# Swapping the halves of rotated heads: four copies on ACT or four transfers

## The chip, the cores and the metric

The kernel runs on one core of a Trainium2 chip, as one launch. The time is that of the device for one execution, in microseconds (us), lower is better. The profiled executions are separate runs, each with its own time. TensorE is called PE in the profile (PEld its weight loads), VectorE DVE, ScalarE ACT, GpSimd POOL; SP is the engine that issues most transfers. Each engine works through its own queue in order and waits for the others at semaphores.

## The reference, cut to what matters

A two-layer model on 256 tokens of width 1024: layer one is a gated recurrence, layer two an attention, each followed by a feed-forward block. The change lies in the attention, where keys and queries are normalised per head (64 channels) and rotated:

```python
def apply_rope(x, cos, sin):
    x1, x2 = jnp.split(x, 2, axis=-1)
    ...
    return jnp.concatenate([x1 * cs - x2 * sn, x2 * cs + x1 * sn], axis=-1)
...
ks = apply_rope(rms_norm(k_sel, k_norm[1]), cos, sin)
kw = apply_rope(rms_norm(k_win, k_norm[2]), cos, sin)
...
q = rms_norm(proj[..., :NSA_Q_WIDTH].reshape(B, S, NSA_HEADS, NSA_HEAD_DIM), q_norm)
q_rope = apply_rope(q, cos, sin)
```

The first half of a head's channels needs the second half at the same token, and the other way round.

## The kernel before, in words

Activations lie with channels on the 128 partitions and the 256 tokens along the free dimension, so a tile of two heads has four blocks of 32 partitions: half, half, half, half. All weights stream from HBM in tiles of 1 MB (`raw`, four buffers, issued on SP's queue in a fixed order, `SCHED`); each is split by ACT into a rounded part (`wh`, L319) and by DVE into the rest (`wl`, L320), and each product is three matmuls (L507 to L509). A raw buffer is loaded anew when whatever read it is done.

The order of the attention's work is written out in the list `ORDER["nsa"]` (L68), but a scheduler sets the final place of each instruction on each engine, by its own costs; the decorator `first` (L187) lends some steps a priority, the rotation a lower one (-15).

The steps that matter here, in the order of the text:

- Keys: two products give `k` for the branches sel and win. ACT writes `hsqk` (squares, L1075) and `huk` (the raw heads, L1076), 128x512 for each branch.
- `rotate` (L1004): `us` gets the heads with the halves swapped (L1010); DVE multiplies the heads by gain and cosine into `KR` or `QR` (L1013), `us` by the swapped gain and the signed sine (L1014), and adds both (L1015). It is called twice for keys (`usk`, `huk`) and four times for queries (`usq`, `huq`), each time for two tiles of two heads.
- `head_norm` (L1017): PE sums the squares (`hs`, L1025); ACT and DVE take the reciprocal root (`hry`, `hrt`, `hrr`, L479 to L486: logarithm, exponent, square, a Newton step), which is split in two (L502, L503); PE spreads it over the channels (`hb`, L1034 and L1035); DVE multiplies (`KR` or `QR`, L1036, and `QN`, L1038). Once for the keys, once for each two query tiles.
- Compression: blocks `Z` (ACT and DVE, L1163 and L1165) and `D` (DVE, L1168) are the stationary side of `cmp` (PE, L1186, 32 matmul records against the two `w1` tiles in `raw`, 32 against `w1late`), whose result runs through a sigmoid (`sg`, `hid`), a transpose (`hidt`), `kc`, `kcsq` (ACT, L1216), `kcms` and `vc`.
- Query tiles: `nq` products; ACT copies them to `huq` (L998) and squares them to `hsqq` (L1000); then rotation and norm. `gates` is a further product, copied to `gu` (L1242) and transposed (`gt`, L1245).
- `v` products (L802 to L804) take `h`, which ACT and DVE compute meanwhile; `css` is the softmax over compressed blocks (L1261 to L1271), its transpose `pct` (PE, L1274); then come the scores `s` (L1291), their maxima and exponents `Pt` (DVE L1296, ACT L452), transposes `ptt` and products `po`. PE fills gaps with `adapsg` and `adapsss` (L408), products for later modulation, fed from `raw` tiles.

Of the kernel before, what the change touches and what calls it, by code (L numbers as in the profile page):

```python
# [186 lines left out]
def first(name):  # L187

    def wrap(f):
        def g(self, *a, **k):  # L190
            n = PRI.get(name, 0)
            if not n:
                return f(self, *a, **k)
            with self.tc.high_priority(offset=n):
                return f(self, *a, **k)
        return g
    return wrap


class K:  # L200
# [802 lines left out]
    @first("rot")  # L1003
    def rotate(self, u, gain, swap, kr, name):  # L1004

        nc = self.nc
        us = self.s2.tile([P, 2, S], F32, tag="us", bufs=2, name=f"us{name}")
        for b in range(4):
            d, e = 32 * b, 32 * (b ^ 1)
            nc.scalar.dma_start(us[d:d + 32], u[e:e + 32])  # L1010
        cs = self.c("cos")[:, None, :].to_broadcast([P, 2, S])
        sn = self.c("sin")[:, None, :].to_broadcast([P, 2, S])
        nc.vector.scalar_tensor_tensor(kr, u, gain, cs, op0=ALU.mult, op1=ALU.mult)  # L1013
        nc.vector.scalar_tensor_tensor(us, us, swap, sn, op0=ALU.mult, op1=ALU.mult)  # L1014
        nc.vector.tensor_tensor(kr, kr, us, op=ALU.add)  # L1015
# [454 lines left out]
```

## Time and profile before

| | |
|---|---|
| median of 3 runs | 744.41 us (742.66 to 746.78) |
| the profiled execution's own time | 748.7 us |
| its span, first to last instruction | 746.9 us |
| mean granted clock of TensorE | 0.986 |
| PE busy | 718.2 us, 96% |
| DVE busy | 587.3 us, 79% |
| ACT busy | 409.7 us, 55% |
| transfers of L1010 | 24 of 64 KB each, issued from 396.68 to 457.28 us |

The profile is of one execution. A timeline row gives start, duration, engine, line and operation, output from input, how many were merged, and in brackets the time that the engine had been idle and what ended it. A waits row gives the waiter, whom it waited for, the sum, how often and the longest. A windows row gives for each stretch its length, the busy time of PE, PEld, DVE, ACT and POOL with the number of instructions, the granted TensorE clock, the share of the transfer engines and GB/s. A group row gives the busy time, the mean duration in ns and the idle time ahead with its releasers. ACTq and SPq are the sequencers of ACT and SP, which issue transfers.

### The profile page before, as it was taken

What the parts mean: (1) busy time and instruction counts of PE and PEld (TensorE: products, weight loads), DVE (VectorE), ACT (ScalarE), POOL (GpSimd) and SP (SyncE); (2) the same over time, 40 slices, a digit from 0 to 9 for tenths busy, and PEclk for the clock granted to TensorE, in tenths of its full rate; (3) what the DMA queues carried; (4) which work ended last, traced back from release to release, by engine and by line L of the source; (5) the groups of instructions that cost most, each with busy time, mean ns of one, the idle gap of its engine ahead of it and who ended that gap; (6) DMA issues with size and microseconds to landing.
All of it is one profiled execution on the core that took longest, in us unless ns stands there. A gap on an engine that the chain in (4) does not pass through costs nothing.

```text
span 746.9 us, 14669 instructions
## 1 busy us (share of the span) xinstructions
PE 718.2 (96%) x5892; PEld 632.0 (85%) x5892; DVE 587.3 (79%) x1221; ACT 409.7 (55%) x796; POOL 0.4 (0%) x5
## 2 busy tenths in 40 slices
PE   3999998999999999999998999999999999999997
PEld 2999986789999999988897797555799888888886
DVE  5996989369899788889677897688689868776642
ACT  4348968267645454544464563757666555565330
POOL 0000000000000000000000000000000000000000
PEclk9999999799999999999999899999999999999999
DMA  8898736555479797889636544455665556756710
GB/s 343 329 351 344 270 109 274 224 226 175 164 283 393 267 362 267 345 307 355 256 131 214 208 160 142 169 195 202 226 221 174 208 188 229 264 183 233 268 43 22
DMA packets 26566, 174.05 MB, mean 233 GB/s; under 512 B 3201, under 2 KB 4609, under 8 KB 6018
## 3 DMA queue, kind: packets, MB, share of 16 engines
q1 hardware_dynamic: 24912, 170.80, 61.8%
q10 hardware_dynamic: 1586, 2.32, 1.0%
q8 instruction: 46, 0.75, 0.4%
q14 instruction: 22, 0.18, 0.1%
HBM read 170.48 MB, written 1.05 MB: 230 GB/s over the span
## 4 chain that ended last, share of the span: by engine, by line
PE 87%; DVE 5%; ACT 3%; DMA 2%; issue 1%; ACTq 0%; DVEq 0%
PE ffo L519 11%; PE ff L507 6%; PE ff L509 6%; PE ff L508 6%; PE ffo L520 6%; PE ff L519 5%; PE po L1348 3%; PE ff L520 2%; PE adapsss L408 2%; PE ptt L1331 2%; PE s L1291 2%; DVE wl L320 1%; PE cmp L1186 1%; PE hg_g L507 1%; PE hg_i L802 1%; PE q L508 1%
## 5 line engine op out<-in xcount | busy, mean ns | idle before, releaser
L319 ACT CAST wh<-raw 128x1024 fp32r<-128x1024 f32 x201 | 208.8, 1049 | 156.1 <-PE ffo L519 47.9
L320 DVE TENSOR_TENSOR wl<-raw,wh 128x1024 fp32r<-128x1024 f32 x201 | 244.4, 1222 | 56.3 <-ACT wh L319 55.4
L519 PE MATMUL ffo<-g,wh 128*128 128x512 f32 x352 | 123.5, 394 | 0.0
L520 PE MATMUL ffo<-g,wl 128*128 128x256 f32 x352 | 99.1, 282 | 0.0
L507 PE MATMUL ff<-hh,wh 128*128 128x256 f32 (+1 forms) x352 | 99.0, 282 | 0.0
L508 PE MATMUL ff<-hl,wh 128*128 128x256 f32 (+1 forms) x352 | 98.8, 281 | 0.0
L509 PE MATMUL ff<-hh,wl 128*128 128x256 f32 (+1 forms) x352 | 98.8, 281 | 0.0
L519 PEld LDWEIGHTS ffo<-g,wh 128*128 128x128 f32 x352 | 66.2, 188 | 15.3
L382 DVE CUSTOM_DVE_ANT_0 junk<-raw,crep 128x1024 f32<-128x1024 f32 x64 | 78.0, 1219 | 0.4
L508 PEld LDWEIGHTS ff<-hl,wh 128*128 128x128 f32 x352 | 66.4, 189 | 0.1
L509 PEld LDWEIGHTS ff<-hh,wl 128*128 128x128 f32 x352 | 66.4, 189 | 0.0
L507 PEld LDWEIGHTS ff<-hh,wh 128*128 128x128 f32 x352 | 66.2, 188 | 0.0
L520 PEld LDWEIGHTS ffo<-g,wl 128*128 128x128 f32 x352 | 66.1, 188 | 0.0
L519 PE MATMUL ff<-h,wh 128*128 128x512 f32 x152 | 54.2, 395 | 0.0
L520 PE MATMUL ff<-h,wl 128*128 128x256 f32 x152 | 42.6, 280 | 0.0
L452 ACT ACTIVATE Pt<-Pt,nm 128x128 f32<-128x128 f32 x64 | 28.2, 443 | 13.7 <-DVE nm L1300 13.6
L519 PEld LDWEIGHTS ff<-h,wh 128*128 128x128 f32 x152 | 28.7, 189 | 6.8 <-DVE h L626 0.2
L677 DVE SCALAR_TENSOR_TENSOR x<-ffo,mod,x 128x256 f32<-128x256 f32 x32 | 15.4, 482 | 18.4 <-PE ffo L520 18.1
L520 PEld LDWEIGHTS ff<-h,wl 128*128 128x128 f32 x152 | 28.6, 188 | 0.0
L502 ACT CAST g<-fg 128x256 fp32r<-128x256 f32 x44 | 17.8, 404 | 17.4 <-DVE fg L971 16.6
L1296 DVE CUSTOM_DVE_ANT_0 Pt<-s,cst 128x128 f32<-128x128 f32 (+1 forms) x64 | 19.0, 351 | 4.1 <-PE s L1291 4.0
L625 ACT ACTIVATE h<-t,mod 128x256 fp32r<-128x256 f32 x16 | 7.7, 506 | 24.1 <-DVE t L624 24.1
(455 smaller groups left out, 1747.0 us busy)
## 6 DMA issues: line engine op xcount, KB each, us to landing
raw<-in_w SPq DMA_DIRECT2D x158, 1024.0 KB, 5.2
w1late<-in_w SPq DMA_DIRECT2D x2, 1024.0 KB, 9.3
x<-in_x SPq DMA_DIRECT2D x2, 512.0 KB, 4.9
usq<-huq ACTq DMA_DIRECT2D x16, 64.0 KB, 4.2
out<-x SPq DMA_DIRECT2D x8, 128.0 KB, 1.9
cst<-in_cst ACTq DMA_DIRECT2D x1, 558.0 KB, 6.9
raw<-in_w SPq DMA_DIRECT2D x1, 512.0 KB, 3.2
usk<-huk ACTq DMA_DIRECT2D x8, 64.0 KB, 6.6
```

What stands on the lines that cost most here:

```text
L319: nc.scalar.copy(wh, u)
L320: nc.vector.tensor_tensor(wl, u, wh.bitcast(F32), op=ALU.subtract)
L382: nc.vector.tensor_tensor_reduce(out=junk, in0=t[:, h * D:(h + 1) * D], in1=self.crep, scale=1.0, scalar=0.0, op0=ALU.mult, op1=ALU.add, a ...
L452: r = nc.scalar.activation(out, in_, func, **kw)
L502: self.nc.scalar.copy(hi, v)
L507: mm(ps, lhsT=wh, rhs=hh, start=first, stop=False)
L508: mm(ps, lhsT=wh, rhs=hl, start=False, stop=False)
L509: return mm(ps, lhsT=wl, rhs=hh, start=False, stop=last)
L519: mm(ps, lhsT=w[k][0], rhs=b, start=k == 0, stop=False)
L520: mm(ps[:, 0], lhsT=w[k][1], rhs=b[:, 0], start=False, stop=k == n - 1)
L1296: nc.vector.tensor_tensor_reduce(out=Pt[half][:, br, o:o + n], in0=ps[half][:, br], in1=cs[:, S - n:], scale=1.0, scalar=-3e38, op0=ALU.ad ...
L1348: nc.tensor.matmul(po[64 * half:64 * half + 64, t], lhsT=w[:, half], rhs=rhs, start=n == 0, stop=n == len(steps) - 1, tile_position=(0, 64 ...
```

## The change

One line of `rotate`. Each of the four blocks of 32 partitions by 512 elements went from `u` to its swapped place in `us` as a transfer issued on ACT's queue; now ACT copies it itself.

```diff
         us = self.s2.tile([P, 2, S], F32, tag="us", bufs=2, name=f"us{name}")
         for b in range(4):
             d, e = 32 * b, 32 * (b ^ 1)
-            nc.scalar.dma_start(us[d:d + 32], u[e:e + 32])
+            nc.scalar.copy(us[d:d + 32], u[e:e + 32])
```

The scheduler then places other instructions differently too; SP's order stays as it was. Four shifts matter to the text. Three are shown, as the rows of the built program give them (line, operation, output from input, size).

ACT, ahead of the key norm's last step on ACT (`hry` from `hrr`), before; `usk_5025` is the second key branch:

```order
L1075 ACTIVATE hsqk_4957<-u,sw 128x256
L1076 ACTIVATE huk_4958<-u,sw 128x256
L452 ACTIVATE hry<-hs,eps 128x256
L1010 DMA usk_5025<-huk_4958 32x512
L452 ACTIVATE hry<-hry 128x256
L1010 DMA usk_5025<-huk_4958 32x512
L482 ACTIVATE hrt<-hry 128x256
L1010 DMA usk_5025<-huk_4958 32x512 x2
L502 CAST hry<-hrr 128x256
L1163 ACTIVATE Z_5075<-u,sw 64x128 x4
```

And now, at the same place:

```order
L319 CAST wh_0_5272<-raw_4966 128x1024
L1075 ACTIVATE hsqk_4957<-u,sw 128x256
L1076 ACTIVATE huk_4958<-u,sw 128x256
L452 ACTIVATE hry<-hs,eps 128x256
L1010 COPY usk_5025<-huk_4958 32x512
L452 ACTIVATE hry<-hry 128x256
L1010 COPY usk_5025<-huk_4958 32x512
L482 ACTIVATE hrt<-hry 128x256
L1010 COPY usk_5025<-huk_4958 32x512 x2
L1163 ACTIVATE Z_5075<-u,sw 64x128 x4
L319 CAST wh_0_5320<-raw_4976 128x1024
L502 CAST hry<-hrr 128x256
```

The four Z operations and two weight casts (5272 is that of `gates`, 5320 the first of the second query tile) stood behind `hry<-hrr` and stand ahead of it now. On PE, nine matmuls of `gates` and two of the second query tile have moved ahead of `hb` along with them, and on DVE both operations that write the second `D` (L1168) stand behind the split of the norm (`hrt`, L503) and ahead of both `hb` multiplies (L1036); before, the first of these and the second key's L1014 stood ahead of them, and that key's L1015 between them. The second key's L1014 and L1015 stand ahead of that split now.

DVE, in the softmax over compressed blocks, before; `usq_5608` is the third query tile's:

```order
L1264 TENSOR_TENSOR css<-css,cmx 128x256
L320 TENSOR_TENSOR wl_1_5729<-raw_5328,wh_1_5728 128x1024
L1266 TENSOR_REDUCE cmx<-css 128x16
L553 CAST hh_6461<-zero 128x8
L554 CAST hl_6462<-zero 128x8
L1267 RECIPROCAL cmx<-cmx 128x16
L1270 TENSOR_TENSOR css<-css,cst 128x256
L1269 TENSOR_TENSOR cmx<-cmx,G 128x16
L1014 SCALAR_TENSOR_TENSOR usq_5608<-usq_5608,cols,cst 128x512
L1271 TENSOR_TENSOR css<-css,cmx 128x256
L1015 TENSOR_TENSOR QR<-QR,usq_5608 128x512
```

And now:

```order
L1264 TENSOR_TENSOR css<-css,cmx 128x256
L1014 SCALAR_TENSOR_TENSOR usq_5608<-usq_5608,cols,cst 128x512
L1266 TENSOR_REDUCE cmx<-css 128x16
L1015 TENSOR_TENSOR QR<-QR,usq_5608 128x512
L1267 RECIPROCAL cmx<-cmx 128x16
L1270 TENSOR_TENSOR css<-css,cst 128x256
L1269 TENSOR_TENSOR cmx<-cmx,G 128x16
L553 CAST hh_6461<-zero 128x8
L554 CAST hl_6462<-zero 128x8
L1271 TENSOR_TENSOR css<-css,cmx 128x256
```

The multiply of `usq` (L1014) stood right ahead of the last `css` step (L1271) and now stands ahead of the sum (L1266).

PE, inside the first `v` product, as the difference (+ is now, - was); `adapsg_5999` is a product whose other 31 matmuls stand far behind, `raw_5494` its weights:

```order
-L804 MATMUL v_5485<-wh_1_5490,h_5234 128x256
+L408 MATMUL adapsg_5999<-raw_5494,c_110 32x256
 L1245 MATMUL gt<-cst,gu 128x128
 L1025 MATMUL hs<-hsqq_5155,cst 32x256 x2
 L1025 MATMUL hs<-hsqq_5381,cst 32x256 x2
 L1245 MATMUL gt<-cst,gu 128x128
+L804 MATMUL v_5485<-wh_1_5490,h_5234 128x256
```

One `adapsg` matmul stands ahead of `gt` and the query norm's `hs` now. Fifteen matmuls of the third query tile that stood ahead of this place are done behind the `v` product instead.

Last, on ACT, three of the second query tile's four copies stand ahead of `kcsq` and the fourth ahead of `gu`; of its transfers two were issued ahead of `kcsq`.

## The prediction

> **What bounds the kernel now.** The page comes first: it says which engine the span is made of.
>
> ```profile
> span 746.9 us, 14669 instructions
> ...
> PE 718.2 (96%) x5892; PEld 632.0 (85%) x5892; DVE 587.3 (79%) x1221; ACT 409.7 (55%) x796; POOL 0.4 (0%) x5
> ...
> usq<-huq ACTq DMA_DIRECT2D x16, 64.0 KB, 4.2
> ...
> usk<-huk ACTq DMA_DIRECT2D x8, 64.0 KB, 6.6
> ```
>
> PE is busy nearly everywhere, so this edit, which takes no matmul away, can only win where PE waits or runs slowly. The 24 transfers take 4.2 and 6.6 us from issue to landing (medians). Next, the longest waits of PE in the stretch 395 to 480 us, where all 24 lie (in total, times, longest):
>
> ```profile
> PE hb L1034 <- ACT hry L502: 3.1, 1, 3.1
> PE pct L1274 <- DVE css L1271: 1.7, 1, 1.7
> PE cmp L1186 <- DVE D L1168: 1.4, 1, 1.4
> ...
> ```
>
> None names a transfer. The timelines of DVE, ACT and PE show what stands behind three of them (start, duration, in brackets the idle time ahead and its releaser):
>
> ```profile
> 406.85 0.75 DVE L1014 SCALAR_TENSOR_TENSOR usk<-usk,cols,cst 128x512 f32<-128x512 f32 x1 [3.39 <-DMA usk<-huk]
> ...
> 412.42 0.75 DVE L1014 SCALAR_TENSOR_TENSOR usk<-usk,cols,cst 128x512 f32<-128x512 f32 x1
> 413.08 0.69 DVE L1168 TENSOR_TENSOR D<-Z,cols 128x512 f32<-128x512 f32 x1
> ...
> 457.39 0.75 DVE L1014 SCALAR_TENSOR_TENSOR usq<-usq,cols,cst 128x512 f32<-128x512 f32 x1 [1.81 <-DMA usq<-huq]
> 458.06 0.42 DVE L1271 TENSOR_TENSOR css<-css,cmx 128x256 f32<-128x256 f32 x1
> ```
>
> ```profile
> 409.54 0.40 ACT L502 CAST hry<-hrr 128x256 fp32r<-128x256 f32 x1 [5.53 <-DMA usk<-huk]
> 409.86 1.66 ACT L1163 ACTIVATE Z<-u,sw 64x128 f32<-64x128 f32 x4
> ...
> 412.01 2.44 ACTq L1010 DMA_DIRECT2D usq<-huq  x4
> ```
>
> ```profile
> 401.73 0.62 PE L1025 MATMUL hs<-hsqk,cst 128*32 128x256 f32 x2 [0.58 <-ACT hsqk L1075]
> ...
> 406.66 0.28 PE L509 MATMUL nq<-hh,wl 128*128 128x256 f32 x1
> 410.00 0.50 PE L1034 MATMUL hb<-hry,rsel 128*128 128x256 f32 x2 [3.06 <-ACT hry L502]
> ...
> 413.82 5.64 PE L1186 MATMUL cmp<-raw,D 128*64 128x256 f32 x29 [1.40 <-DVE D L1168]
> ...
> 419.31 3.83 PE L1186 MATMUL cmp<-w1late,D 128*64 128x256 f32 x31
> ```
>
> ACT and DVE stand in order behind transfers that have not landed: the key norm waits behind them, so hb does; D and css stand behind a usk or usq multiply in DVE's queue. Last, the windows view, in steps of 3.41 us laid on the two dips of the granted clock (PEclk is the number ahead of the DMA share):
>
> ```profile
> 404.63:408.05 3.42, 2.31 (x20) 2.10 (x18) 1.16 (x2) 0.00 (x0) 0.00 (x0) 1.00 1.00 349
> 408.05:411.46 3.41, 1.46 (x7) 1.00 (x8) 1.76 (x5) 1.88 (x6) 0.00 (x0) 1.00 0.27 82
> 411.46:414.87 3.41, 2.01 (x11) 1.35 (x12) 3.05 (x5) 1.39 (x4) 0.00 (x0) 0.50 0.24 58
> 414.87:418.29 3.42, 3.42 (x20) 1.90 (x18) 3.42 (x6) 2.56 (x3) 0.00 (x0) 0.50 0.08 19
> 455.83:459.24 3.41, 1.68 (x15) 1.28 (x14) 1.84 (x4) 0.08 (x1) 0.00 (x0) 1.00 0.93 335
> 459.24:462.65 3.41, 3.34 (x13) 1.91 (x10) 2.88 (x17) 0.00 (x0) 0.00 (x0) 0.50 0.05 13
> ```
>
> A window with 1.40 us of idle PE or more (3.41 less 2.01, 1.46 or 1.68) is followed by one at half clock; one with 1.11 us (3.42 less 2.31) is not. So the waits are paid twice.
>
> **The change part by part.** *Price of a copy.* No row shows 32 partitions by 512 from SBUF. The ACT groups of the stretch, by form:
>
> ```profile
> L319 ACT CAST wh<-raw 128x1024 fp32r<-128x1024 f32 x16 | 16.6, 1050 | 7.7 <-PE nq L508 3.2 <-DMA usq<-huq 2.0 <-PE kv L508 1.7
> ...
> L1163 ACT ACTIVATE Z<-u,sw 64x128 f32<-64x128 f32 x8 | 3.3, 407 | 1.0 <-DVE u L668 0.9
> ...
> L502 ACT CAST hh<-t 128x256 fp32r<-128x256 f32 x8 | 2.9, 403 | 0.7 <-DVE t L639 0.6
> ...
> L998 ACT COPY huq<-nq 128x512 f32<-128x512 f32 x4 | 2.3, 575 | 1.6 <-PE nq L509 1.6
> ```
>
> Between 256 columns (403 ns) and 1024 (1050 ns) the straight line gives 0.62 us at 512. Four Z copies, which change partitions, take 1.66 us (4 x 0.407 is 1.63), so I let nothing overlap and take 0.62. The low end is 0.48 (the 575 ns copy with the roughly 0.1 us by which neighbours on ACT overlap); the high end 1.05, the cast of double length, should moving across partitions halve the rate. All 24: 14.9 us of ACT. Four are 2.5 us where ACT's queue took 2.44 us to issue four transfers, so ACT is held no longer than before; what goes is the landing.
>
> *hs and hb.* ACT's rows ahead of the key norm:
>
> ```profile
> 397.32 0.16 ACT L667 COPY sw<-k 128x1 f32<-128x1 f32 x1 [0.68 <-ACT huk L1076]
> ...
> 398.19 0.52 ACT L1075 ACTIVATE hsqk<-u,sw 128x256 f32<-128x256 f32 x1 [0.71 <-DVE u L668]
> ...
> 399.64 0.16 ACT L667 COPY sw<-k 128x1 f32<-128x1 f32 x1 [0.23 <-issue]
> ...
> 401.17 0.51 ACT L1075 ACTIVATE hsqk<-u,sw 128x256 f32<-128x256 f32 x1 [1.37 <-DVE u L668]
> ```
>
> Four copies and the moved gates cast (2.48 + 1.05 = 3.53) fill 2.99 us of idle here (0.68 + 0.71 + 0.23 + 1.37): hsqk, and hs with it, come 0.54 later, and PE's wait of 0.58 becomes 1.12. hs ended at 402.35 (401.73 + 0.62) and now ends at 402.89. From there ACT does three functions of hry (0.42 each), four copies (2.48), Z (1.66) and the nq cast (1.05) before the hry cast: 6.45 us, so that starts at 409.34 instead of 409.54, and hb, 0.46 behind it, at 409.80. PE, 0.54 later with its nq row (free at 407.32), now has nine gates matmuls first (9 x 0.12 = 1.07, to 408.39), waits for the nq cast (to 409.34), does two matmuls (0.24) and waits for hb: 1.17 us idle instead of 3.06. Both waits together: 3.64 to 2.29, a gain of **1.35**. It is ACT, no longer a transfer, that is late next.
>
> *cmp.* In DVE's queue the first hb multiply and the second key's L1014 stood ahead of D. Now that key's work is done while ACT works towards hry, and D stands right behind hrt's split (L503), which starts with hry's cast done, at 409.74: half a microsecond of L503 and one D operation of 0.69 end near 410.8, while PE does hb until about 411. Gain **1.40**, with little cover: 0.2 us.
>
> *First dip.* 29 records at 5.64/29 = 0.194 us against 3.83/31 = 0.124 at full clock: 29 x 0.071 = **2.05**, if no window idles 1.40 us any more.
>
> *pct.* The usq multiply moves ahead of the exponent's sum in DVE's queue, and its data comes 2.5 us of copies behind huq instead of a landing; ACT, which does css's exponent too, idles there and has room for both. The wait of 1.74 us goes: **1.74**. Late next are the nq matmuls, after which the v matmuls fill PE until css is done.
>
> *Second dip.* Eight s records in the dip and eight at full clock:
>
> ```profile
> 458.90:461.32 2.42, 2.42 (x8) 1.67 (x10) 0.57 0.18 44
> 468.06:469.45 1.39, 1.39 (x8) 0.68 (x8) 1.00 0.00 0
> ```
>
> 2.42 - 1.39 = **1.03**; these feed DVE's maxima and the exponents that PE waits for later, and the next eight overlap with DVE, so I count one set. The Trainium skill, "TensorE: Matmul & The Clock Gate", section "Part 1: The HAM clock gate", lets the clock fall to half after an idle window of about 3.4 us. By that rule a window half busy, like 455.83 to 459.24, should not count and the sum would be 1.03 smaller; the row shows half clock behind it, and the row decides.
>
> *What the copies cost.* Three of them now stand ahead of kcsq, which had only 1.02 us of idle before it (ACT's, PE's and SP's timelines, and the landings of weight loads between 415 and 440 us):
>
> ```profile
> 433.70 0.23 ACT L1216 ACTIVATE kcsq<-kc 128x64 f32<-128x64 f32 x1 [1.02 <-PE kc L1213]
> ...
> 438.11 0.27 PE L1245 MATMUL gt<-cst,gu 128*128 128x128 f32 x1
> ...
> 431.24 0.33 SPq L296 DMA_DIRECT2D raw<-in_w  x1
> ...
> DMA to landing us min/median/max: 4.9/9.2/12.0
> ```
>
> 3 x 0.62 - 1.02 = 0.84 later, and one more copy (0.62) ahead of gu; PE's v matmuls, which covered both, need h casts from the same queue. Bounds 0 and 1.46; I take **1.2** lost, near the upper, as 15 nq matmuls that filled PE here move behind.
>
> *At nothing:* SP's order is unchanged; raw buffers come free earlier because the gates cast does (cover: the transfers landed in time before). Without the cover, a wait for weights, see below.
>
> Sum: 1.35 + 1.40 + 2.05 + 1.74 + 1.03 - 1.2 = **6.4 us**. The profiled execution took 748.7 us (span 746.9) and would take 742.3; it was 4.3 us above the median of the three runs (742.66 to 746.78), so I take the difference off the median: 744.4 - 6.4 = **738.0 us**.
>
> **The rivals.**
>
> *Copies at the upper bound.* At 1.05 us, eight of them ahead of hb add 8 x 0.43 = 3.4 us to that wait, the first dip stays (2.05), and kcsq and gu lose another 1.7: 6.4 - 7.2 = -0.8, **745.2 us**, no change. For it: the rows at hand have other shapes. Against: the Z copies change partitions at no visible price.
>
> *The clock stays low.* The new wait at hs (1.12) and that at hb (1.17) lie between the 1.11 that did no harm and the 1.40 that did. Then 2.05 stays lost: **740.1 us**, still faster.
>
> *The second dip has another cause.* Should the half clock at 459.24 come of something else than the half-idle window ahead of it, it stays: **739.0 us**. That is how the Trainium skill's clock-gate section would have it; four windows of this trace speak against it, three idle ones and one that was not idle enough.
>
> *Slower: a matmul ahead of its weights.* One adapsg matmul (L408) moves from far behind into the middle of the v product, just ahead of gt and hs. PE serves in order. Its raw tile was issued only at 431.24, and loads of that stretch took 4.9 to 12.0 us to land. By then the kernel has gained 3.6 us (1.35 + 1.40 + 2.05 - 1.2), and the 15 nq matmuls that move behind are another 1.8, so gt's place comes near 432.7 (438.11 - 5.4). The load's buffer comes free with the last v weights, which gain the 3.6 and some 1.5 more, as their own raw tile is loaded earlier: issue near 426. At 4.9 us it lands at 431, in time. At 12.0 it lands at 438, PE idles 5.3 us, and two windows at half clock lose up to 3.4: 6.4 - 8.7 = -2.3, **746.7 us**; it decides once the landing takes over 9.7 us (3.0 us idle and the 3.4 are the whole gain), and with copies at their upper bound too it makes 754. Against it: three loads, not four, queue together then.
>
> **How the numbers follow.** Forecast 0.58; copies at the upper bound, or another loss that ACT's load gives back, 0.17; clock stays low 0.13; the second dip's other cause 0.05; weights late 0.07. About 0.5% (3.7 us) is what a measurement of this kernel can tell from no change, so faster means under 740.7 us, slower over 748.1. The clock's rival lies 0.6 us inside that bound, so two thirds of it count as faster (0.09), with the forecast and the second dip's other cause: 0.72. Of late weights most counts as slower, since its price has no firm upper end, 0.05; the rest, 0.23, is no change. Range: downward, copies at 0.48 save 8 x 0.14 = 1.1 at hb and a cover without loss 1.2, which gives 735.7, and about 1 us more if the last wait of the list, 0.58 at hs, also goes with a ready hsqk: 734.5. Upward it takes in the clock's rival and most of the way to the first: 743.5.
>
> **What would show it.** Right: no wait of ACT or DVE for usk or usq; PE's wait at hb about 1.2 us and at cmp none; PEclk 1.00 from 405 to 425 and near 455; ACT's busy time up by 15 us; L1010 at 0.62 us. Wrong: L1010 near 1 us, PEclk still 0.50 behind hb, a wait of PE at adapsg or kcms of several us, or gt at an unchanged 438.1 us (about 432.7 expected).

## The result, and the profile after

The changed kernel takes 741.16 us (median of eight runs, 738.19 to 742.57), the kernel before, in the runs beside it, 747.00 (eight runs, 742.66 to 749.11): a ratio of 0.9923, 95% interval 0.9894 to 0.9951, or 5.8 us. In a second measurement (the last run below), with other runs of the kernel before, it was 0.9889 (0.9854 to 0.9923). The forecast was 6.4 us less, 738.0 us, with a range of 734.5 to 743.5. The measured time lies in it, 3.2 us above the forecast; 2.6 of these come from the kernel before, which takes 747.00 us here and took 744.41 in the three runs that the forecast started from. The profiled execution took 741.87 us. Its page begins:

```profile
span 740.1 us, 14648 instructions
...
PE 716.4 (97%) x5892; PEld 631.1 (85%) x5892; DVE 586.5 (79%) x1221; ACT 424.6 (57%) x820; POOL 0.4 (0%) x5
```

ACT is busy 14.9 us longer (409.7 before), what 24 copies of 0.62 us make. PE's waits in the same stretch, 395 to 480 us:

```profile
PE nq L507 <- ACT wh L319: 1.0, 1, 1.0
PE hs L1025 <- ACT hsqk L1075: 1.0, 1, 1.0
PE s L1291 <- DVE mx L1296: 0.4, 1, 0.4
```

hb, pct and cmp are gone from the list, and so is a wait of 0.6 at ptt. ACT, DVE and PE around the key norm, one timeline each:

```profile
404.88 1.24 ACT L1010 COPY usk<-huk 32x512 f32<-32x512 f32 x2
406.15 1.68 ACT L1163 ACTIVATE Z<-u,sw 64x128 f32<-64x128 f32 x4
407.85 1.04 ACT L319 CAST wh<-raw 128x1024 fp32r<-128x1024 f32 x1
408.80 0.40 ACT L502 CAST hry<-hrr 128x256 fp32r<-128x256 f32 x1
```

```profile
406.56 0.74 DVE L1014 SCALAR_TENSOR_TENSOR usk<-usk,cols,cst 128x512 f32<-128x512 f32 x1
...
409.24 0.43 DVE L503 TENSOR_TENSOR hrt<-hrr,hry 128x256 fp32r<-128x256 f32 x1 [0.99 <-ACT hry L502]
409.58 1.29 DVE L1168 TENSOR_TENSOR D<-Z,cols 128x512 f32<-128x512 f32 x2
```

```profile
408.95 0.39 PE L507 MATMUL nq<-hh,wh 128*128 128x256 f32 x1 [1.03 <-ACT wh L319]
...
411.23 3.52 PE L1186 MATMUL cmp<-raw,D 128*64 128x256 f32 x29
...
431.62 0.33 PE L1245 MATMUL gt<-cst,gu 128*128 128x128 f32 x1
```

ACT does the hry cast without idle time ahead of it (5.53 us before); the second key's L1014 waits for nothing; the 29 cmp records take 3.52 us instead of 5.64; gt comes 6.49 us earlier. The windows view shows the clock:

```profile
408.16:411.57 3.41, 2.62 (x16) 2.00 (x18) 2.29 (x5) 3.38 (x7) 0.00 (x0) 1.00 0.64 267
411.57:414.98 3.41, 3.41 (x34) 3.18 (x32) 3.41 (x6) 3.12 (x4) 0.00 (x0) 1.00 0.00 0
452.54:455.95 3.41, 2.95 (x10) 1.07 (x8) 3.33 (x21) 1.60 (x5) 0.00 (x0) 1.00 0.00 0
455.95:459.36 3.41, 3.41 (x15) 3.12 (x15) 2.46 (x13) 3.41 (x17) 0.00 (x0) 0.50 0.00 0
```

The dip behind hb is gone. The one near 456 us is still there in this profile, now behind a window with only 0.46 us idle.

### The profile page after: what moved, and what is told of

Its sections match the earlier page's. It is cut to its first block, busy times and chain, and to the rows that moved or that the text cites. A ratio compares the mean times of both kernels' runs of the same rounds, so it can differ in the third digit from the quotient of the medians.

```text
span 740.1 us, 14648 instructions
## 1 busy us (share of the span) xinstructions
PE 716.4 (97%) x5892; PEld 631.1 (85%) x5892; DVE 586.5 (79%) x1221; ACT 424.6 (57%) x820; POOL 0.4 (0%) x5
## 3 DMA queue, kind: packets, MB, share of 16 engines
HBM read 170.48 MB, written 1.05 MB: 232 GB/s over the span
## 4 chain that ended last, share of the span: by engine, by line
PE 88%; ACT 5%; DVE 4%; issue 1%; DMA 1%; ACTq 0%
PE ffo L519 11%; PE ff L507 6%; PE ff L509 6%; PE ff L508 6%; PE ffo L520 6%; PE ff L519 5%; PE po L1348 3%; PE adapsss L408 2%; PE ff L520 2%; PE ptt L1331 2%; PE s L1291 2%; PE q L508 1%; PE hg_i L802 1%; PE hg_g L507 1%; DVE wl L320 1%; PE nso L507 1%
```

## The experiments

Times are medians; each ratio is to the runs of the kernel before made beside it (747.1 to 747.8 us). Where an edit adds lines, later lines are numbered one or two higher in its rows.

**Keys alone.**

```diff
-            nc.scalar.dma_start(us[d:d + 32], u[e:e + 32])
+            (nc.scalar.copy if name[0] == "k" else nc.scalar.dma_start)(us[d:d + 32], u[e:e + 32])
```

> The keys' eight blocks are copied by ACT, the queries' sixteen stay transfers. Theory (a landing that stands in the in-order queues of ACT and DVE is what cost the time): PE's waits at hb (3.1 us in the profile of before) and cmp (1.4) go or shrink as in the changed kernel, where hs and nq took 1.0 each, the clock stays at 1.00 from 405 to 425 us, and DVE still waits for a usq transfer ahead of the last css step, so a wait of PE at pct of 1 to 2 us stays. Gain 1.35 + 1.40 + 2.05 = 4.8 us by the prediction's terms, of the changed kernel's 5.8 (747.0 to 741.2): about 742 us. Rival (the time came from the queries' part, or from fewer transfers in all): 745 to 747 us, with hb still waited for or the clock still at 0.50 behind it.

Measured: 747.56 us, ratio 1.0006 (0.9990 to 1.0023), no gain. Yet the keys' stage did what the theory said: hs and nq wait 1.0 us each, hb and cmp not at all, and the clock never falls there. Against the expectation the wait at pct is gone too: in this order no usq multiply of DVE waits for its transfer. PE has no new wait of over 0.7 us; it works longer. In the groups of PE from 450 to 532 us (busy time, mean ns), first of before, then of this run:

```profile
L1348 PE MATMUL po<-PT,V 128*64 128x256 f32 (+1 forms) x127 | 15.5, 335 | 0.0
L408 PE MATMUL adapsss<-raw,c 128*32 128x512 f32 x64 | 9.4, 603 | 0.0
L1348 PE MATMUL po<-PC,VC 128*64 128x256 f32 x32 | 7.3, 395 | 0.0
...
L1025 PE MATMUL hs<-hsqq,cst 128*32 128x256 f32 x8 | 0.6, 391 | 0.0
```

```profile
L1348 PE MATMUL po<-PT,V 128*64 128x128 f32 (+1 forms) x128 | 17.2, 337 | 0.0
L408 PE MATMUL adapsss<-raw,c 128*32 128x512 f32 x64 | 12.3, 602 | 0.0
L1348 PE MATMUL po<-PC,VC 128*64 128x256 f32 x32 | 8.0, 395 | 0.0
...
L1025 PE MATMUL hs<-hsqq,cst 128*32 128x256 f32 x8 | 2.5, 391 | 0.0
```

At nearly the same mean durations these groups are busy 2.9 + 1.9 + 1.7 + 0.7 = 7.2 us longer, because fewer of their records overlap. A record also overlaps with its neighbours of other groups, so the time lost by this is at most 7.2 us. PE's timeline of before and of this run at the second query norm:

```profile
472.50 0.64 PE L1025 MATMUL hs<-hsqq,cst 128*32 128x256 f32 x8
```

```profile
462.31 0.62 PE L1025 MATMUL hs<-hsqq,cst 128*32 128x256 f32 x2
462.86 0.33 PE L1331 MATMUL ptt<-cst,Pt 128*128 128x128 f32 x1
463.11 0.62 PE L1025 MATMUL hs<-hsqq,cst 128*32 128x256 f32 x2
```

Four 32-column matmuls in a row (two records each) take 0.64 us, one alone 0.62. The scheduler, with other costs to place, had strewn hs, adapsss and po among others. So "keys alone" was not one change, and the next run undoes the other.

**Keys alone, in another order.** As above, and

```diff
-PRI = {"gates": -100, "av": 10, "res": 60, "rot": -15, "fh": 60}
+PRI = {"gates": -100, "av": 10, "res": 60, "rot": -30, "fh": 60}
```

> Keys copied and queries transferred as in the run that copied only the keys, but with the rotation's priority at -30 instead of -15, by which PE's order after the keys has the groupings of before: the second query norm's four hs matmuls stand together again (in the run with keys alone they stood apart, 0.62 us each, 2.48 instead of 0.64), and adapsss falls into nine steps of about 1 us again instead of twelve. Theory (the keys' copies bring nearly the whole gain, and a scattered order in the scores took it back): 747.6 less 1.8 (hs) less 2.9 (adapsss) less about 0.6 (s) = 742 us, with hs and nq waited for 1.0 us each and no wait at hb and cmp; with the wait at pct left, up to 743.5. Rival (the keys' copies bring nothing, whatever the order): 746 to 748 us.

Measured: 742.40 us, 0.9928 (0.9903 to 0.9954). hs is back at 0.6 us and adapsss at 9.4 in the same group view. PE's waits from 395 to 480 us:

```profile
PE pct L1274 <- DVE css L1271: 1.8, 1, 1.8
PE hs L1025 <- ACT hsqk L1075: 1.3, 1, 1.3
...
```

As expected: the keys' copies bring 4.8 of the 5.8 us, and the wait at pct stays, since a usq transfer holds up DVE for 2.0 us again.

**Keys alone, hs together.** The first run once more, with only hs held together:

```diff
-                nc.tensor.matmul(ps[e:e + 32], lhsT=self.c("sel"), rhs=sq[:, m], start=True, stop=True,
-                                 tile_position=(0, e))
+                with self.tc.high_priority(offset=10):
+                    nc.tensor.matmul(ps[e:e + 32], lhsT=self.c("sel"), rhs=sq[:, m], start=True, stop=True,
+                                     tile_position=(0, e))
```

> The run that copied only the keys (747.6 us) once more, with one thing added: the hs matmuls of head_norm get a priority 10 higher, by which the second query norm's four stand together again, as before, instead of one by one between ptt matmuls; the rotation's priority stays at -15. adapsss falls into ten steps of about 1 us by this order, instead of twelve (nine in before). Theory (the keys' copies' gain was taken back by the scattered order of PE's 32-column matmuls): hs takes 0.64 us instead of 2.48 and adapsss 2 us less: 747.6 - 1.8 - 2.0 = 743.7 us, 742.5 to 745. Rival (it was the rotation's other priority, not the grouping, that gave the 742.4 us): 746.5 to 748 us.

Measured: 742.69 us, 0.9942 (0.9918 to 0.9966). In its groups from 450 to 532 us:

```profile
L408 PE MATMUL adapsss<-raw,c 128*32 128x512 f32 x64 | 9.6, 597 | 0.0
...
L1026 PE MATMUL hs<-hsqq,cst 128*32 128x256 f32 x8 | 1.0, 388 | 0.0
```

2.7 + 1.5 us less than in the first run, and the time fell by 4.9. So the rotation's priority was not needed, and these two groups account for most of what the first run had lost. The po groups are still longer (17.1 and 8.4 us), and whether that still costs time is not shown. The sixteen query transfers hold up no multiply of DVE here, as in the first run, and PE does not wait at pct: for that wait another order was enough, without copies.

**Queries alone.**

```diff
+            (nc.scalar.copy if name[0] == "q" else nc.scalar.dma_start)(us[d:d + 32], u[e:e + 32])
```

> The other half alone: the queries' sixteen blocks are copied, the keys' eight stay transfers. Theory: PE's wait at hb stays near 3.1 us, at cmp near 1.4, and the clock is 0.50 behind them as before; only the wait at pct (1.74) goes. With the second dip left where the changed kernel has it, the gain is 1.7 us or a little less: 745 to 746 us. Rival (the queries carry the gain): 742 to 743 us. If both halves together give more than the whole (5.8 us), one wait was paid in either; if less, the copies of one part undo some of the other.

Measured: 745.42 us, 0.9968 (0.9949 to 0.9986), 2.4 us. Its waits in the same stretch:

```profile
PE hb L1034 <- ACT hry L502: 3.3, 1, 3.3
PE cmp L1186 <- DVE D L1168: 1.4, 1, 1.4
...
```

pct is gone, hb and cmp are as before: the theory, with a little more gain than its 1.7. The two halves (4.8 and 2.4) add up to the whole within the intervals.

**Each block copied twice.** The line of the copy stands twice.

> Each block is copied twice to the same place, so ACT has 24 more copies of 0.62 us, 14.9 us in all; nothing else is done more. In the order that the scheduler gives, eleven copies stand ahead of the key norm's last cast instead of eight, but the Z copies and two weight casts (1.66 + 2.1 us) stand behind it, so hb should come no later than in the changed kernel; D stands behind the late Z copies and five more copies, so cmp waits anew. Theory that ACT is what is late next around hb and cmp: a new wait of PE at cmp of 2 to 4 us and a dip of the clock with 2 us behind it, and a further 1 to 2 us ahead of kcsq and gu: 745 to 749 us. Rival (ACT, at 55% busy, has room and the price of a copy does not matter): within 1 us of the changed kernel, 741 to 742 us.

Measured: 755.20 us, 1.0088 (1.0055 to 1.0122); its profiled execution was one of the quickest, 750.5. The direction is the theory's, the size beyond it. PE's longest wait from 395 to 480 us:

```profile
PE cmp L1187 <- DVE D L1169: 4.6, 1, 4.6
...
```

The named wait came and was longer than named. Two copies are 1.24 us for each block, a little over the prediction's upper bound of 1.05, and they undo the change and more, in an order of their own. That ACT is busy only 57% of the time in the changed kernel is no room where hb and D are due.

**Half on DVE.**

```diff
+            (nc.scalar.copy if b < 2 else nc.vector.tensor_copy)(us[d:d + 32], u[e:e + 32])
```

> Two of the four blocks are copied by ACT and two by DVE, to see whether ACT's length is what PE still waits for at hs and nq (1.0 us each in the profile of the changed kernel). Theory that it is: both waits shrink by about a microsecond in all where ACT has four copies less ahead of hb, and since DVE (79% busy) gets twelve copies of 0.4 to 0.7 us, 5 to 8 us in all, part comes back in the softmax: 740 to 742 us. Rival (the two waits are set by the chain of the norm, not by the copies): no gain, 741 to 744 us, the waits as they were.

Measured: 741.67 us, 0.9917 (0.9892 to 0.9943), like the changed kernel. The waits of 1.0 us at hs and nq shrank to one of 0.6 at hb, and waits for DVE of 0.8 at hs and 0.6 at s came: half of each theory, and no gain.

**Transfers, with the multiply later.** No copies; in the kernel before, `"rot": -15` becomes `"rot": -40`.

> No copies at all: the 24 transfers as before, only the rotation's priority goes from -15 to -40, by which DVE's order puts both D operations and the norm's split ahead of every usk multiply, and css ahead of the usq multiply. Theory (it is the place of the waiting multiply in DVE's queue that costs, not the transfer): no wait of PE at cmp and pct, hb waited for 1 us or less, clock 1.00 behind it: a gain like the copies', 5 to 6 us, less about 1 us since adapsss falls into one more step: 742 to 743.5 us. Rival (the landing itself, or the transfers' traffic, costs): the waits move to hb's multiply or the scores and the time is 745 to 748 us.

Measured: 748.17 us, 1.0021 (1.0001 to 1.0040). PE's longest wait in the stretch, and DVE's timeline:

```profile
PE hidt L1201 <- DVE hid L1193: 4.6, 1, 4.6
```

```profile
420.22 0.75 DVE L1014 SCALAR_TENSOR_TENSOR usq<-usq,cols,cst 128x512 f32<-128x512 f32 x1 [3.82 <-DMA usq<-huq]
```

hb, cmp and pct wait no more, as the theory said, but the sum came out as its rival did: the landing now holds up DVE ahead of the sigmoid, hidt waits, and the granted clock is 0.50 for 6.8 us from 423.2 us on.

**Transfers out of the way.**

```diff
             n = PRI.get(name, 0)
+            if name == "rot":
+                n = -40 if a[4][0] == "k" else -100 if a[4] in ("q0", "q1") else -60
```

> All 24 transfers again, as in the run with later transfers (748.2 us), where the waits at hb, cmp and pct had gone and one of 4.6 us at hidt had come: the first usq multiply stood ahead of the sigmoid's steps in DVE's queue and waited 3.8 us for its landing. Here the priority is -40 for the keys' rotation, -100 for the first two query tiles' and -60 for the last two, by which that multiply stands behind the sigmoid's last step and css's last step ahead of the third tile's multiply. Theory (a landing costs only by what stands behind the waiting multiply in DVE's queue): the 4.6 us at hidt go, with the half clock behind it, 748.2 - 4.6 = 743.6 us or up to 2 us less: 741.5 to 744 us, like the copies. Rival (the transfers cost in some other way, as by their traffic beside the weight loads): another wait takes its place, 746 to 749 us.

Measured: 751.13 us, 1.0038 (1.0017 to 1.0059). The rival again; PE from 439 to 480 us, and DVE:

```profile
PE s L1293 <- DVE mx L1298: 4.4, 1, 4.4
```

```profile
460.07 0.75 DVE L1016 SCALAR_TENSOR_TENSOR usq<-usq,cols,cst 128x512 f32<-128x512 f32 x1 [4.06 <-DMA usq<-huq]
```

The wait at hidt is gone and stands among the maxima of the scores. In the kernel before and in these two orders DVE stands still for two landings each (3.4 and 1.8 us, 4.4 and 3.8, 4.5 and 4.1), and at least one of them keeps PE waiting. The Trainium skill, "DMA: Bandwidth & Descriptors", section "Rules for kernel authors", advises to issue a transfer early and wait for it late. By that rule both runs should have matched the copies; they agree only as far as the old waits went. Late enough would be a place with as much DVE work ahead of it as the landing lasts, and neither order had one for every tile. Keys alone, with hs together or not, had one for all four query multiplies.

**Copies, later.** The changed kernel with `"rot": -40`.

> The partner of the run with later transfers: the copies of the changed kernel with the rotation's priority at -40; the order of PE's 32-column groups is nearly the same as there. Theory (with nothing queued behind a landing, copies have no advantage, and their 14.9 us load ACT, which is late at hs and nq): the same as the later transfers within 1 us or up to 2 us slower, 742 to 744 us. Rival (copies are better in themselves, by fewer transfers beside the weight loads or a shorter path): 2 us or more faster than the later transfers.

Measured: 742.78 us, 0.9940 (0.9916 to 0.9964): 5.4 us faster than the transfers at the same priority. The rival: at this priority the gain belongs to the copies, not to the order.

**Keys on GpSimd.**

```diff
+            (nc.scalar.copy if name[0] == "q" else nc.gpsimd.tensor_copy)(us[d:d + 32], u[e:e + 32])
```

> The keys' eight blocks are copied by GpSimd, which is idle (0.4 us busy before), the queries' sixteen by ACT. Theory that ACT's copies ahead of hs and of the nq cast cost the 1.0 us at each: both waits shrink to the 0.6 of before or less, and if a GpSimd copy takes under 1.5 us, usk is in time for the multiply behind D: 1 to 1.5 us gained on the changed kernel's 741.2 less about 1 us for one more adapsss step, 740 to 742 us. Rival (a GpSimd copy is slow, 2 us or more, or slows DVE beside it): DVE waits for usk ahead of the norm's split, hb is late by several us: 744 to 750 us.

Measured: 740.22 us, 0.9912 (0.9881 to 0.9942), not to be told from the changed kernel. The waits at hs are 0.6 at most, but hb waits again, 1.7 us.

**All on GpSimd, and the changed kernel again.** `nc.gpsimd.tensor_copy` for all, `"rot": -30`; and the changed kernel unedited.

> All 24 copies on GpSimd (median 0.69 us each for the keys' eight in the run where it copied those), with the rotation's priority at -30, by which the second query norm's hs matmuls stay together. Theory that ACT's load is what is left of the price: with 9.9 us less of ACT than in the run with only the keys on GpSimd (740.2 us), 739 to 740.5 us. Rival (nothing of the queries' part waits for ACT's copies; the order decides): 740 to 742 us, and slower than the changed kernel if a GpSimd copy holds up DVE.

> The changed kernel itself once more, unedited, beside the other two on the same chip: 741.2 us within 1 us, so that the two can be compared with it directly.

Measured: 746.55 us, 0.9983 (0.9960 to 1.0006), and 740.01. Four copies in a row on GpSimd take 3.2 to 3.7 us, and DVE is slow beside them; the timelines of GpSimd and DVE in this run:

```profile
409.51 3.44 POOL L1010 COPY usq<-huq 32x512 f32<-32x512 f32 x4 [2.36 <-ACT huq L998]
```

```profile
407.22 0.67 DVE L1168 TENSOR_TENSOR D<-Z,cols 128x512 f32<-128x512 f32 x1
...
409.62 1.09 DVE L1168 TENSOR_TENSOR D<-Z,cols 128x512 f32<-128x512 f32 x1
410.63 0.82 DVE L486 TENSOR_TENSOR hrr<-hrt,hry 128x256 f32<-128x256 f32 x1
```

The same D operation takes 0.67 us without and 1.09 with a copy beside it, hrr 0.82 instead of 0.42 in the changed kernel. hb waits 2.8 us and pct 1.5. What came is the rival's last clause, slower because GpSimd holds up DVE, at a larger price than either theory's range. The unedited kernel lies 1.2 us below the expected 741.2, 0.2 beyond the margin of 1 us.

## Why the prediction was right, and where not

- *Price of a copy.* 0.62 us, no overlap, as taken (two in a row 1.24). The rival at 1.05 us fell with it.
- *hs and hb.* 2.29 us were forecast to remain; 1.00 and 1.03 remain, with ACT late in both, as said. The gain is 3.64 - 2.03 = 1.61 instead of 1.35.
- *cmp and first dip.* 1.40 and 5.64 - 3.52 = 2.12, as forecast (1.40, 2.05). The clock did not stay low.
- *pct.* The 1.74 went. That the copies are needed for it is not shown: with only the keys copied it also went, by the order alone. The 0.6 us at ptt, which the sum left out, went with it.
- *What the copies cost.* 1.2 us were booked, and nothing was lost there: kcsq ran at 427.52 right behind its three copies, and kcms at 427.79 with no wait in PE's list, as PE had v matmuls until then. That term was mis-sized.
- *Second dip.* The step that failed: that without the wait at pct the half clock would be gone, and that the half clock costs the s matmuls 1.03 us. PE's timeline, before and after:

```profile
458.90 5.37 PE L1291 MATMUL s<-KR,QR 64*128 64x256 f32 x16
```

```profile
451.07 3.61 PE L1291 MATMUL s<-KR,QR 64*128 64x256 f32 x14
455.10 1.21 PE L1291 MATMUL s<-KR,QR 64*128 64x512 f32 x2 [0.42 <-DVE mx L1296]
456.62 0.41 PE L803 MATMUL v<-wl,h 128*128 128x256 f32 x1
...
458.97 0.41 PE L802 MATMUL v<-wh,h 128*128 128x256 f32 x1
```

The sixteen s records take 455.10 + 1.21 - 451.07 = 5.24 us, nearly all at full clock; before, with 3.4 us of them at half clock, they took 5.37. At full clock it is DVE, busy for 3.33 us of the window 452.54 to 455.95, that they wait for. And the dip, still there, now falls on v matmuls: from 456.62 the eleventh further one starts at 458.97, every 0.21 us instead of 0.12, and some thirteen such steps of 0.09 make about 1.2 us. Instead of a gain of 1.03 this is a loss of 1.1.

The second profile of the changed kernel, of the run with nothing edited, does not have this dip. Its s matmuls start at 450.05, and at the v matmuls behind them the clock is 1.00 (a timeline row, then two windows):

```profile
454.08 1.09 PE L1291 MATMUL s<-KR,QR 64*128 64x512 f32 x2 [0.42 <-DVE mx L1296]
453.88:457.29 3.41, 3.21 (x20) 2.48 (x21) 3.13 (x21) 3.03 (x14) 0.00 (x0) 1.00 0.00 0
457.29:460.70 3.41, 3.41 (x29) 3.21 (x30) 2.29 (x6) 3.41 (x17) 0.00 (x0) 1.00 0.00 0
```

Here the records take 454.08 + 1.09 - 450.05 = 5.12 us, all at full clock: the gain is 0.25 us, not 1.03. So the prediction's rival of 5%, that the dip stays, came in one profile of the two. A wait at pct can bring the half clock all the same: with the keys in another order, where PE still waits 1.8 us there, a window with 1.59 us of PE busy ends at 450.49 and half clock follows.

Sum by measured terms, first profile: 1.61 + 1.40 + 2.12 + 1.74 + 0.6 - 1.1 = 6.4 us. The two spans differ by 6.8, of which 0.7 is there already when the first hs starts (399.03 before, 398.33 now), ahead of the change, so 6.1 are to be explained. So the total is right by luck in part: a cost of 1.2 us that did not come and a gain at the second dip that came out 2.1 us smaller cancel in part, and small terms make up the rest. In the second profile the sum is 1.61 + 1.40 + 2.12 + 1.74 + 0.6 + 0.25 = 7.7 us; from the first hs (397.30) to the end the spans differ by 347.9 - 340.3 = 7.6. The mechanism of the larger part, landings in in-order queues, is shown by the waits that went, by the two runs in which only the keys were copied and hs stood together, and by the pair at priority -40. The slower rival did not come: PE never waits at adapsg.

What stays open: why the window 452.54 to 455.95, with 2.95 us of PE busy, is followed by half clock in one profile of this kernel. No run was aimed at it. Whether fewer transfers beside the weight loads help in themselves was not tried apart either.

## What to carry to other kernels

A transfer inside the core that something in an in-order queue waits for costs its landing, unless the queue has that much other work ahead of the wait. In two runs moving the wait down the queue only changed who paid; in two others the order left the query transfers enough time. Price the copy that replaces it on the stretch where it falls, not by the engine's average load. And where a scheduler places instructions, compare the groups' busy times before believing an experiment: an edit of one stage can scatter narrow matmuls in another and hide its own gain.

## What the runs showed of the hardware that was not expected

- Narrow matmuls overlapped only where they stood next to each other: one adapsss matmul of 32 columns (two records) or four in a row take the same time, here in the run with keys alone:

```profile
487.84 1.06 PE L408 MATMUL adapsss<-raw,c 128*32 128x512 f32 x8
...
492.01 1.04 PE L408 MATMUL adapsss<-raw,c 128*32 128x512 f32 x2
```

- The clock fell behind windows in which PE was busy for half of the time. Two pairs of neighbouring windows of the run with the keys on GpSimd:

```profile
406.11:409.52 3.41, 2.11 (x12) 1.52 (x14) 3.06 (x7) 2.54 (x5) 0.00 (x0) 1.00 0.00 0
409.53:412.94 3.41, 3.41 (x32) 3.20 (x34) 3.41 (x6) 0.82 (x2) 0.00 (x0) 1.00 0.00 0
133.05:136.46 3.41, 1.78 (x50) 1.48 (x50) 2.90 (x8) 0.21 (x1) 0.00 (x0) 1.00 1.01 423
136.47:139.88 3.41, 3.41 (x92) 2.93 (x81) 0.00 (x0) 0.82 (x4) 0.00 (x0) 0.50 0.93 370
```

Laid on the dips' grid in the profiles of before, after and the twelve experiments, all 20 full-clock windows with PE busy for up to 1.8 us (from 20 to 730 us) are followed by half clock, and of the 17 with 1.8 to 2.3 us three are. Above that there are two, one with 2.95 us in the changed kernel and one with 2.56 in the run with transfers out of the way. The bound of the prediction, 1.40 us idle, was too low: it is about 1.6, with exceptions. Its window of 1.40 was itself at half clock already. The Trainium skill, "TensorE: Matmul & The Clock Gate", section "Part 1: The HAM clock gate", speaks of an idle window of about 3.4 us; the length agrees, but here a half-busy one is enough. The grid lies differently against the kernel in each execution: in the two profiles of the changed kernel dips start at 124.85, 138.51 and 455.95 us in the first and, up to 730 us, only at 136.44 in the second. So the same program can have a dip in one execution and none in the next.
